# Hybrid trunk layer: another order of the query and key stage, part of its DMAs on POOL's queue, and the latents in eleven pieces

## Chip, core and metric

One core of a Trainium2 chip. The metric is the device time of one execution in microseconds, given as the median of three runs. TensorE is called PE, VectorE DVE, ScalarE ACT, GpSimd POOL and SyncE SP, as in the profile.

## What is computed

One layer with three branches (a Fourier mix, a gated delta rule scan, latent attention) that are merged by gates. The change touches the merge of the first two branches and the stage that makes queries, keys and values for the third. Cut to that:

```python
q = (rmsnorm(cq, q_norm) @ w_uq).reshape(B, L, 8, 64 + 32)      # cq: 1024 x 384
kv = (rmsnorm(ckv, kv_norm) @ w_ukv).reshape(B, L, 8, 64 + 64)  # ckv: (1024 + 256) x 256
q_nope, q_pe = q[..., :64], q[..., 64:]
k_nope, v = kv[..., :64], kv[..., 64:]
q_pe, kpe = apply_rope(q_pe, cos, sin), apply_rope(kpe, cos, sin)   # rope for the 1024, not the 256
# attention of 1024 queries over 1280 keys, 8 heads of 96
p = softmax(einsum('bqhd,bkhd->bhqk', q, k) * 96 ** -0.5)
merged = sigmoid(g_a) * (y_a @ w_branch[0]) + sigmoid(g_b) * (y_b @ w_branch[1]) + sigmoid(g_c) * (y_c @ w_branch[2])
```

All data is fp32. A product of two fp32 matrices is made of three matmuls on operands that are split into a high and a low part (high·high, high·low, low·high).

## The kernel before

**Order of work.** A planner orders the instructions of each engine from their dependencies and the program's order; it may let an instruction of a queue go ahead of one that stands earlier in the program. Where `self.fine` is true (the query and key stage and the attention), the matmuls keep the program's order, and so do the DVE instructions that are given to `pin`. Every engine and every DMA queue then works through its list in order: an instruction that waits holds up all behind it.

**Merge.** `merge_ab` runs m over eight tiles of the merged width. For each m it loads two weights (`wload`: SP loads, ACT makes the high part, POOL the low part), makes two products `pb` (b = 0 and 1, each 24 matmuls into one of two PSUM buffers), multiplies each by its gate on DVE (L1239; this frees the PSUM buffer), adds them on POOL (L1240) and stores the sum (L1241). At the end of m = 1 to 7 it takes one step of the generator `latents`, which prepares the third branch: `rows` (the norms' factors), the rope of the key's shared 32 dimensions (three pieces, stored in `kpd`), the normed key latents `ckh`/`ckl` and query latents `cqh`/`cql` (in `hilo`: DVE scales, ACT makes the high part, DVE the low part), and the values' weight. Each step issues its own loads into `cs` (three buffers) on SP's queue just ahead of the work on them.

**Query and key stage.** `qkv` makes tiles from the latents: `k_tile` (1280 columns in chunks of 512, 512 and 256; six matmuls a chunk), `qn_tile` (1024 columns in two chunks of nine matmuls), `qp_tile` (the rope part of the queries, four chunks of nine), `v_tile` (six matmuls). Each chunk of keys or queries goes through `put`: ACT copies the high part out of PSUM, DVE subtracts for the low part, and both are stored to DRAM, the high part from ACT's queue and the low part from SP's (L1366; four buffers `csh` and `csl`). From DRAM they come back in the layout of the attention: `k_pe` fills the shared 32 rows of the key tiles (one row of ones and eight DMAs, L1353 and L1357), `load_k` (L1424) and `load_q` (L1432, L1433) the others, all on SP's queue. `peak` makes one of the 20 pieces of the score maximum of the first query block: one matmul `s` into one of two PSUM buffers (two of half the width for the last four pieces), and one DVE maximum (L1448, L1454). `shift` joins them, and ACT writes the result into a row of the query tile (`Q<-sh`, L1466). The order before is: key tile 0, queries 0 (both parts), six value tiles, two maxima, key tile 1, three maxima, queries 1, four, key tile 2, three, queries 2, five, key tile 3, three, `shift`, queries' rope part 1, queries 3, four value tiles.

**Attention.** `attend` starts with the scores of the first block (`st<-Q,K`), and runs the maxima of the next block beside them; POOL adds up the weights.

Of the kernel before, what the change touches and what calls it, by code (L numbers as in the profile page):

```python
# [162 lines left out]
class K:  # L163
# [1023 lines left out]
    def merge_ab(self):  # L1187
        nc, tc, a = self.nc, self.tc, self.a
        with ExitStack() as es:
# [65 lines left out]
    def latents(self):  # L1255
# [3 lines left out]
        def cs(w):  # L1259
            return lp.tile([P, L], FP32, name="cs", bufs=3)[:, 0:w]  # L1260
# [15 lines left out]
        pieces = [(b, min(b + 512, LT)) for b in range(0, LT, 512)]  # L1276
        for b, e in pieces:
            w = e - b
            k = cs(2 * w)[0:32].rearrange("p (h c) -> p h c", h=2)
# [8 lines left out]
            hl = lp.tile([32, 2, 512], F32R, name="kphl", bufs=1)[:, :, 0:w]  # L1288
# [4 lines left out]
        self.ckh, self.ckl = (lp.tile([P, 2, LT], F32R, name=n) for n in ("ckh", "ckl"))  # L1293
        for b, w in ((0, L), (L, LC)):
            rb = cs(w)
            nc.sync.dma_start(out=rb, in_=rows[0][:, b:b + w].broadcast_to([P, w]))
            for k in range(2):
                st = cs(w)
                nc.sync.dma_start(out=st, in_=self.ckvd[k][:, b:b + w])
                self.hilo(st, self.kvn[:, k:k + 1], rb, self.ckh[:, k, b:b + w], self.ckl[:, k, b:b + w])  # L1300
            yield
        self.cqh, self.cql = (lp.tile([P, 3, L], F32R, name=n) for n in ("cqh", "cql"))
        rb = cs(L)
        nc.sync.dma_start(out=rb, in_=rows[1].broadcast_to([P, L]))
        for t in range(3):
            st = cs(L)
            nc.sync.dma_start(out=st, in_=self.cqd[t])
            self.hilo(st, self.qn_g[:, t:t + 1], rb, self.cqh[:, t, :], self.cql[:, t, :])
            if t == 0:
                yield  # L1310
        yield
        self.wvh, self.wvl = (lp.tile([P, 2, 512], F32R, name=n) for n in ("wvh", "wvl"))
        st = cs(L).rearrange("p (k c) -> p k c", k=2)
        nc.sync.dma_start(out=st, in_=self.a["wuv"])
        self.split(st, self.wvh, self.wvl)
        yield

    def qkv(self):
# [6 lines left out]
        with ExitStack() as es:  # L1325
# [3 lines left out]
            def cst(w):  # L1329
                return self.lp.tile([P, L], FP32, name="cs", bufs=3)[:, 0:w]  # L1330
# [56 lines left out]
            n = 0  # L1387

            def peaks(m):
                nonlocal n  # L1390
                for _ in range(m):
                    self.peak(0, n)
                    n += 1
# [23 lines left out]
            for t in range(VF, 10):  # L1417
                v_tile(t)
# [3 lines left out]
    def load_k(self, t):  # L1422
        for k, src in zip(self.Kt[t % 2], self.knd):
            self.nc.sync.dma_start(out=k[0:64].bitcast(FP32), in_=src[t].rearrange("(p d) l -> d p l", p=2))  # L1424

    def load_q(self, j):
# [4 lines left out]
        for q, n, p in zip(self.Qt[j], self.qnd, self.qpd):  # L1431
            nc.sync.dma_start(out=q[0:64].bitcast(FP32), in_=n[t].rearrange("(p d) l -> d p l", p=2)[:, :, bs])  # L1432
            nc.sync.dma_start(out=q[64:96].bitcast(FP32),  # L1433
# [35 lines left out]
    def attend(self):  # L1469
# [5 lines left out]
        with ExitStack() as es:  # L1475
# [58 lines left out]
            for j in range(NB):  # L1534
                more = j + 1 < NB
                n = 0
                if j % 2 == 0 and j + 2 < NB:
                    self.load_k(j // 2 + 1)
                if j + 2 < NB:
                    self.load_q(j + 2)  # L1540
# [131 lines left out]
```

## Time and profile before

| | us |
|---|---|
| median of three runs | 1612.68 (1611.36 to 1612.69) |
| profiled execution, its own time | 1606.86 |
| its span | 1605.1 |
| merge, first `pb` to last `pb` | 1014.6 to 1116.3 |
| query and key stage, to the first scores of the attention | 1116.7 to 1219.7 |
| PE busy over the span | 94% |
| mean granted clock of PE | 0.973 |

How to read it: PE is the engine with the most work, and the chain of work that ended last runs mostly over PE. A stage's time is PE's matmuls at the full clock, plus what PE waited, plus what the matmuls lost while the clock was granted at its lower level (half). The mean busy share hides this: a matmul at the lower level counts as busy all the same.

### The profile page before, as it was taken

To read this page: it belongs to the slowest core of one execution; us is meant where nothing else is said; L and a number is where in the kernel's file an instruction comes from. 1 tells how busy PE (TensorE), PEld (TensorE's weight loads), DVE (VectorE), ACT (ScalarE), POOL (GpSimd) and SP (SyncE) were. 2 spreads that over 40 slices of the span, in tenths; PEclk is the share of its full clock that TensorE was granted. 3 is DMA by queue.
4 is the path that set the end of the run, shared out by engine and by line. 5 is a ranking of instruction groups with operands and counts; after the bars stand their busy time and mean duration, and the time that the engine had idled before them with its cause. 6 is when DMAs were issued, how large, how long until landed. Compare 5 with 4: busy or idle time off the path is not lost.

```text
span 1605.1 us, 20192 instructions
## 1 busy us (share of the span) xinstructions
PE 1513.2 (94%) x7403; PEld 1185.2 (74%) x7403; DVE 794.1 (49%) x1489; ACT 545.1 (34%) x1158; POOL 564.4 (35%) x462
## 2 busy tenths in 40 slices
PE   6989999999899999999999999899679898999998
PEld 1676788888788878788788888777457565666886
DVE  2756665454343256345443123544245566756724
ACT  3455324322332433433432334122124343443311
POOL 0464242212235435443443221444005465653000
PEclk9899999999999999999999999999879999999999
DMA  8522222311332123224223226585862312103715
GB/s 322 164 59 74 83 69 88 121 47 67 118 96 92 56 73 118 77 74 144 57 86 108 77 79 209 165 282 183 217 203 86 76 30 60 27 14 125 230 37 180
DMA packets 93103, 179.35 MB, mean 112 GB/s; under 512 B 21510, under 2 KB 26568, under 8 KB 92748
## 3 DMA queue, kind: packets, MB, share of 16 engines
q1 hardware_dynamic: 81980, 158.82, 31.9%
q10 hardware_dynamic: 11024, 19.24, 3.3%
q8 instruction: 58, 0.95, 0.3%
q14 instruction: 41, 0.34, 0.1%
HBM read 125.60 MB, written 52.38 MB: 111 GB/s over the span
## 4 chain that ended last, share of the span: by engine, by line
PE 71%; DVE 6%; DMA 6%; issue 2%; ACT 2%; POOL 1%; SPq 1%; ACTq 0%; DVEq 0%; POOLq 0%
PE mm L175 31%; PE st L175 10%; PE pp L175 7%; PE pf L175 5%; PE g L175 5%; PE acc L175 4%; PE pb L175 3%; PE pm L175 2%; PE s L175 2%; DVE tmp L746 1%; DMA Q<-sh 1%; DMA ys<-in_wmod 1%; DMA Q<-qph 1%; PE g L182 1%; DVE N L748 1%
## 5 line engine op out<-in xcount | busy, mean ns | idle before, releaser
L197 POOL TENSOR_TENSOR wl<-wr,wh 128x512 fp32r<-128x512 f32 x142 | 195.8, 1380 | 544.6 <-ACT wh L196 527.7
L175 PE MATMUL mm<-hhi,wh 128*128 128x512 f32 x912 | 375.2, 411 | 1.4 <-ACT st L1075 1.0
L175 PE MATMUL mm<-hhi,wl 128*128 128x512 f32 x912 | 360.0, 395 | 0.0
L175 PE MATMUL mm<-hlo,wh 128*128 128x512 f32 x912 | 358.0, 393 | 0.0
L175 PEld LDWEIGHTS mm<-hhi,wl 128*128 128x128 f32 x912 | 172.1, 189 | 37.6
L175 PEld LDWEIGHTS mm<-hhi,wh 128*128 128x128 f32 x912 | 173.0, 190 | 32.7 <-ACT st L1075 1.4
L175 PEld LDWEIGHTS mm<-hlo,wh 128*128 128x128 f32 x912 | 173.2, 190 | 31.4 <-issue 0.8
L196 ACT CAST wh<-wr 128x512 fp32r<-128x512 f32 (+2 forms) x154 | 93.4, 608 | 202.4 <-PE mm L175 104.8
L175 PE MATMUL st<-Q,K 96*128 96x512 f32 (+1 forms) x480 | 139.6, 407 | 10.0 <-DMA Q<-sh 9.6
L1487 ACT ACTIVATE pf<-st 128x512 f32<-128x512 f32 x160 | 94.6, 597 | 130.1 <-PE st L175 127.6
L1448 DVE TENSOR_REDUCE mx<-s 128x1 f32<-128x512 f32 x128 | 86.6, 690 | 79.4 <-PE s L175 79.2
L175 PEld LDWEIGHTS st<-Q,K 96*128 96x128 f32 (+1 forms) x480 | 89.0, 193 | 45.3 <-DMA Q<-sh 12.4
L1496 POOL TENSOR_TENSOR sum<-sum,pf 128x512 f32<-128x512 f32 x94 | 117.8, 1284 | 3.2 <-ACT pf L1487 3.0
L175 PE MATMUL s<-K,Q 96*128 96x512 f32 (+1 forms) x192 | 63.5, 376 | 17.8 <-DMA Q<-qph 9.6
L175 PE MATMUL acc<-pf,V 128*64 128x512 f32 x320 | 72.2, 597 | 0.0
L175 PEld LDWEIGHTS s<-K,Q 96*128 96x128 f32 x192 | 36.7, 194 | 30.8 <-DVE mx L1448 11.1
L175 PE MATMUL pb<-yh,wh 128*128 128x512 f32 x128 | 51.8, 405 | 7.6 <-DVE t L1239 7.6
L878 POOL TENSOR_TENSOR Qm<-mk,Qf 128x128 f32<-128x128 f32 x64 | 31.9, 519 | 69.0 <-PE g L175 67.1
L175 PEld LDWEIGHTS acc<-pf,V 128*64 128x64 f32 x320 | 21.5, 136 | 42.1 <-issue 42.1
L869 DVE SCALAR_TENSOR_TENSOR S<-S,ex,g 128x128 f32<-128x128 f32 x48 | 15.2, 344 | 73.5 <-PE g L175 73.4
L175 PE MATMUL pb<-yh,wl 128*128 128x512 f32 x128 | 51.0, 398 | 0.0
L175 PE MATMUL pb<-yl,wh 128*128 128x512 f32 x128 | 51.0, 398 | 0.0
(392 smaller groups left out, 2725.9 us busy)
## 6 DMA issues: line engine op xcount, KB each, us to landing
wr<-in_win SPq DMA_DIRECT2D x118, 256.0 KB, 2.7
wm<-in_wmod SPq DMA_DIRECT2D x16, 512.0 KB, 7.0
tabd<-st ACTq DMA_DIRECT2D x24, 256.0 KB, 2.0
wr<-in_wbr SPq DMA_DIRECT2D x24, 256.0 KB, 4.4
t<-tabd SPq DMA_DIRECT2D x12, 512.0 KB, 3.9
xt<-in_xT SPq DMA_DIRECT2D x8, 640.0 KB, 10.9
wm<-in_win SPq DMA_DIRECT2D x8, 512.0 KB, 4.0
kqd<-lk SPq DMA_DIRECT2D x8, 512.0 KB
```

The costliest lines, as they stand in the source:

```text
L175: i = self.nc.tensor.matmul(out, lhsT, rhs, start=start, stop=stop)
L182: i = self.nc.tensor.transpose(out=out, in_=in_, identity=identity)
L196: nc.scalar.copy(out=hi, in_=raw)
L197: self.lo_eng.tensor_tensor(out=lo, in0=raw, in1=hi, op=ALU.subtract)
L746: nc.vector.tensor_tensor(out=tv, in0=XX[:, i:i + 1, i + 1:16].broadcast_to([P, m, m]), in1=N[:, i + 1:16, i + 1:16].rearrange("p k j -> p ...
L748: nc.vector.tensor_reduce(out=N[:, i, i + 1:16], in_=tv, axis=AX.X, op=ALU.add)
L869: nc.vector.scalar_tensor_tensor(out=Sn[:, dr], in0=S[:, dr], scalar=eL(dr), in1=sp[:, dr], op0=ALU.mult, op1=ALU.add)
L878: nc.gpsimd.tensor_tensor(out=Qm[:, dr], in0=self.mk[:, m_, :], in1=Qf[:, c[dr], :], op=ALU.mult)
L1448: self.pin(nc.vector.tensor_reduce(out=mx[:, i, c:c + 1], in_=ps, axis=AX.X, op=ALU.max))
L1487: nc.scalar.activation(out=pf, in_=ps, func=AF.Exp)
L1496: nc.gpsimd.tensor_tensor(out=out, in0=s[0], in1=pf, op=ALU.add)
```

## The change

- In the merge, a step of `latents` is taken at the end of every m and, from m = 1 on, another after the matmuls of b = 0, ahead of that product's gate on DVE. `latents` has eleven pieces of work in place of six, and each piece is followed by the issue of the next one's loads; `cs` has four buffers in place of three.
- In the query and key stage the order is: queries 0 (both parts), key tile 0, the shared key rows, the loads of key tile 0 and of query blocks 0 and 1, six value tiles; then for t = 1, 2, 3 key tile t, and for t = 1, 2 queries t, two value tiles and four maxima. `k_tile` and `qn_tile` make one maximum with each chunk, ahead of its `put`, while there are any. After `shift`: the queries' rope part 1, queries 3.
- The stores of the low parts, the eight DMAs and the row of `k_pe`, and these first loads of keys and queries are issued from POOL's queue in place of SP's. Later loads stay on SP's queue.

```diff
                     for c in range(2):
                         s = slice(c * 512, (c + 1) * 512)
                         self.mm3(ps[:, s], hi, lo, ...)
+                    if b == 0 and m:
+                        next(pieces, None)
                     nc.vector.scalar_tensor_tensor(out=g, in0=g, scalar=1.0, in1=ps, op0=ALU.add, op1=ALU.mult)
...
-                if m:
-                    next(pieces)
+                next(pieces, None)
...
+        def rope_load(b, e):
+            k = t["k", b] = cs(2 * (e - b))[0:32].rearrange("p (h c) -> p h c", h=2)
             if b < L:
                 nc.sync.dma_start(out=k, in_=self.kped.rearrange("(h p) l -> p h l", p=32)[:, :, b:e])
-                r = cs(2 * w)[0:32].rearrange("p (h c) -> p h c", h=2)
-                nc.sync.dma_start(out=r, in_=self.a["ropek"].rearrange("(h p) l -> p h l", p=32)[:, :, b:e])
-                nc.vector.tensor_tensor(out=k, in0=k, in1=r, op=ALU.mult)
-                nc.vector.tensor_tensor(out=k[:, 0], in0=k[:, 0], in1=k[:, 1], op=ALU.add)
+                t["r", b] = cs(2 * (e - b))[0:32].rearrange("p (h c) -> p h c", h=2)
+                nc.sync.dma_start(out=t["r", b], in_=self.a["ropek"].rearrange("(h p) l -> p h l", p=32)[:, :, b:e])
...
+        def row_load(i, b, w):
+            t["row"] = cs(w)
+            nc.sync.dma_start(out=t["row"], in_=rows[i][:, b:b + w].broadcast_to([P, w]))
+
+        def lat_load(src, key):
+            t[key] = cs(src.shape[-1])
+            nc.sync.dma_start(out=t[key], in_=src)
...
+        work = [(lambda b=b, e=e: rope_load(b, e), lambda b=b, e=e: rope_do(b, e)) for b, e in ((0, 512), (512, L), (L, LT))]
+        for b, w in ((0, L), (L, LC)):
+            for k in range(2):
+                load = lambda k=k, b=b, w=w: lat_load(self.ckvd[k][:, b:b + w], ("ck", k, b))
+                work.append((both(lambda b=b, w=w: row_load(0, b, w), load) if k == 0 else load,
+                             lambda k=k, b=b, w=w: ck_do(k, b, w)))
+        for k in range(3):
+            load = lambda k=k: lat_load(self.cqd[k], ("cq", k))
+            work.append((both(lambda: row_load(1, 0, L), load) if k == 0 else load, lambda k=k: cq_do(k)))
+        work.append((wv_load, lambda: self.split(t["wv"], self.wvh, self.wvl)))
+        work[0][0]()
         yield
...
+        for i, (_, do) in enumerate(work):
+            do()
+            if i + 1 < len(work):
+                work[i + 1][0]()
             yield
...
-                nc.sync.dma_start(out=self.Kt[1][0][KR:KR + 1].bitcast(FP32), in_=row)
+                nc.gpsimd.dma_start(out=self.Kt[1][0][KR:KR + 1].bitcast(FP32), in_=row)
...
-                            nc.sync.dma_start(out=self.Kt[b][i][64:KR, par].bitcast(FP32), in_=self.kpd[:, i])
+                            nc.gpsimd.dma_start(out=self.Kt[b][i][64:KR, par].bitcast(FP32), in_=self.kpd[:, i])
...
-                nc.sync.dma_start(out=dst[1][:, c:c + w], in_=lo.bitcast(FP32))
+                nc.gpsimd.dma_start(out=dst[1][:, c:c + w], in_=lo.bitcast(FP32))
 
             def k_tile(t):
                 for c, d, ps in up_tile(a["wuk"][t], 2, ckh, ckl, LT):
+                    peaks()
                     put(ps, [x[t] for x in self.knd], c)
 
             def qn_tile(t):
                 for c, d, ps in up_tile(a["wuq"][t], 3, cqh, cql, L):
+                    peaks()
                     put(ps, [x[t] for x in self.qnd], c)
...
-            k_tile(0)
             qn_tile(0)
             qp_tile(0)
+            k_tile(0)
             k_pe()
+            self.load_k(0, nc.gpsimd)
+            self.load_q(0, nc.gpsimd)
+            self.load_q(1, nc.gpsimd)
             for t in range(VF):
                 v_tile(t)
-                if t == 2:
-                    self.load_k(0)
-                    self.load_q(0)
-            peaks(2)
+            on = True
             for t in range(1, 4):
                 k_tile(t)
-                peaks(3)
-                if t == 1:
-                    self.load_q(1)
                 if t < 3:
                     qn_tile(t)
-                    peaks(4 if t == 1 else 5)
+                    for i in range(2):
+                        v_tile(VF + 2 * (t - 1) + i)
+                        peaks(2)
+            peaks(20)
             self.shift(0)
             qp_tile(1)
             qn_tile(3)
-            for t in range(VF, 10):
-                v_tile(t)
```

## Rows read from the trace of the kernel before

**Rows 1.** By stretch: us, busy us of PE, PEld, DVE, ACT, POOL, granted clock, DMA share, GB/s.
```profile
1014.60:1116.30 101.70, 94.12 (x391) 73.00 (x390) 49.11 (x50) 18.57 (x30) 42.76 (x24) 0.98 0.63 210
1116.30:1219.70 103.40, 80.28 (x302) 61.76 (x301) 42.44 (x66) 24.61 (x47) 8.71 (x5) 0.85 0.68 201
...
1140.99:1150.95 9.96, 0.33 (x2) 0.00 (x0) 0.00 (x0) 0.59 (x1) 0.00 (x0) 0.76 1.01 207
1150.95:1199.15 48.20, 35.04 (x116) 26.00 (x117) 24.09 (x41) 10.10 (x20) 0.00 (x0) 0.78 0.75 222
...
1219.70:1256.00 36.30, 36.30 (x160) 24.49 (x159) 22.46 (x34) 17.47 (x30) 22.27 (x18) 1.00 0.17 47
```
**Rows 2.** Waits in the merge, then in the stage: us, times, longest.
```profile
DVE cs L1251 <- DMA cs<-ckvd: 9.0, 2, 7.0
PE pb L175 <- DVE t L1239: 7.6, 4, 3.3
...
PE s L175 <- DMA Q<-qph: 9.6, 1, 9.6
PE s L175 <- DVE mx L1448: 6.5, 5, 1.7
PE st L175 <- ACT wh L196: 4.0, 1, 4.0
PE s L175 <- DVE mx L1454: 1.6, 1, 1.6
```
**Rows 3.** Chain of work in the stage: start us, us, what.
```profile
1116.67 16.04 PE st L175 x72
1132.70 1.40 PE acc L175 x6
...
1138.95 0.67 SPq L1424
...
1140.99 9.92 DMA Q<-qph
```
**Rows 4.** Timeline of PE: a chunk of 256 columns, and the transposition of `shift`.
```profile
1119.40 0.28 PE L175 MATMUL st<-ckl,wh 128*128 128x256 f32 x1
1119.52 0.28 PE L175 MATMUL st<-ckh,wl 128*128 128x256 f32 x1
...
1198.78 0.38 PE L182 MATMUL ms<-mk,m 128*8 128x128 f32 x1 [1.00 <-DVE m L1461]
```
**Rows 5.** Waits of SP's queue, 1014 us to 1222 us.
```profile
SPq L1366 <- DVE csl L1364: 37.3, 17, 6.0
```
**Rows 6.** Instructions of the low parts `csl`: time to landing.
```profile
DMA to landing us min/median/max: 2.0/3.6/4.3
```
**Rows 7.** DMA issues from 1116 us to 1160 us: sizes.
```profile
K<-knh SPq DMA_DIRECT2D x1, 640.0 KB
...
Q<-qnh SPq DMA_DIRECT2D x2, 256.0 KB
...
Q<-qph SPq DMA_DIRECT2D x2, 128.0 KB
```
**Rows 8.** Timeline of POOL, the stage's beginning: start us, us, what.
```profile
1120.71 2.23 POOL L1352 MEMSET K<- 1x2560 f32 x1
```
**Rows 9.** Instructions of the query tiles: time to landing.
```profile
DMA to landing us min/median/max: 3.9/5.8/9.7
```
**Rows 10.** By line in the stage: names, shapes xcount | busy us, mean ns | idle.
```profile
L1364 DVE TENSOR_TENSOR csl<-st,csh 128x512 fp32r<-128x512 f32 x16 | 11.0, 691 | 21.1 <-ACT csh L1363 19.5 <-DMA knl<-csl 1.5
L1448 DVE TENSOR_REDUCE mx<-s 128x1 f32<-128x512 f32 x16 | 10.4, 685 | 15.3 <-PE s L175 15.1
...
L197 POOL TENSOR_TENSOR wl<-wr,wh 128x512 fp32r<-128x512 f32 x3 | 3.9, 1293 | 92.6 <-ACT wh L196 92.6
```
**Rows 11.** Chain of work in the attention: a wait for the row that `shift` stores.
```profile
1273.02 8.22 DMA Q<-sh
```
**Rows 12.** Timeline of PE, merge: the first of its four waits.
```profile
1026.99 0.47 PE L175 MATMUL pb<-yh,wh 128*128 128x512 f32 x1 [1.00 <-DVE t L1239]
```

More of the change, by code (lines that the diff above doesn't have):

```diff
@@ L1259, in cs @@
         def cs(w):
-            return lp.tile([P, L], FP32, name="cs", bufs=3)[:, 0:w]
+            return lp.tile([P, L], FP32, name="cs", bufs=4)[:, 0:w]
         rows = []
@@ L1275, in latents, with rope_do @@
         yield
[L1276 to L1279, printed above, removed]
+        t = {}
+        def rope_load(b, e):
+            k = t["k", b] = cs(2 * (e - b))[0:32].rearrange("p (h c) -> p h c", h=2)
             if b < L:
                 nc.sync.dma_start(out=k, in_=self.kped.rearrange("(h p) l -> p h l", p=32)[:, :, b:e])
-                r = cs(2 * w)[0:32].rearrange("p (h c) -> p h c", h=2)
-                nc.sync.dma_start(out=r, in_=self.a["ropek"].rearrange("(h p) l -> p h l", p=32)[:, :, b:e])
-                nc.vector.tensor_tensor(out=k, in0=k, in1=r, op=ALU.mult)
-                nc.vector.tensor_tensor(out=k[:, 0], in0=k[:, 0], in1=k[:, 1], op=ALU.add)
+                t["r", b] = cs(2 * (e - b))[0:32].rearrange("p (h c) -> p h c", h=2)
+                nc.sync.dma_start(out=t["r", b], in_=self.a["ropek"].rearrange("(h p) l -> p h l", p=32)[:, :, b:e])
             else:
                 nc.sync.dma_start(out=k[:, 0], in_=self.kped[0:32, b:e])
-            hl = lp.tile([32, 2, 512], F32R, name="kphl", bufs=1)[:, :, 0:w]
+        def rope_do(b, e):
+            k = t["k", b]
+            if b < L:
+                nc.vector.tensor_tensor(out=k, in0=k, in1=t["r", b], op=ALU.mult)
+                nc.vector.tensor_tensor(out=k[:, 0], in0=k[:, 0], in1=k[:, 1], op=ALU.add)
+            hl = lp.tile([32, 2, 512], F32R, name="kphl", bufs=1)[:, :, 0:e - b]
             nc.scalar.copy(out=hl[:, 0], in_=k[:, 0])
@@ L1291, in latents @@
             nc.scalar.dma_start(out=self.kpd[:, :, b:e], in_=hl.bitcast(FP32))
-        yield
[L1293 to L1300, printed above, removed]
-            yield
@@ L1302, in latents @@
[L1302 to L1316, printed above, removed]
+        self.ckh, self.ckl = (lp.tile([P, 2, LT], F32R, name=n) for n in ("ckh", "ckl"))
+        self.cqh, self.cql = (lp.tile([P, 3, L], F32R, name=n) for n in ("cqh", "cql"))
+        self.wvh, self.wvl = (lp.tile([P, 2, 512], F32R, name=n) for n in ("wvh", "wvl"))
+        def row_load(i, b, w):
+            t["row"] = cs(w)
+            nc.sync.dma_start(out=t["row"], in_=rows[i][:, b:b + w].broadcast_to([P, w]))
@@ new lines, in lat_load, with ck_do, cq_do, wv_load @@
+        def lat_load(src, key):
+            t[key] = cs(src.shape[-1])
+            nc.sync.dma_start(out=t[key], in_=src)
+        def ck_do(k, b, w):
+            self.hilo(t["ck", k, b], self.kvn[:, k:k + 1], t["row"], self.ckh[:, k, b:b + w], self.ckl[:, k, b:b + w])
+        def cq_do(k):
+            self.hilo(t["cq", k], self.qn_g[:, k:k + 1], t["row"], self.cqh[:, k, :], self.cql[:, k, :])
+        def wv_load():
+            t["wv"] = cs(L).rearrange("p (k c) -> p k c", k=2)
+            nc.sync.dma_start(out=t["wv"], in_=self.a["wuv"])
@@ new lines, in both @@
+        def both(*fs):
+            return lambda: [f() for f in fs]
+        work = [(lambda b=b, e=e: rope_load(b, e), lambda b=b, e=e: rope_do(b, e)) for b, e in ((0, 512), (512, L), (L, LT))]
[4 more added lines that the diff above has]
+                             lambda k=k, b=b, w=w: ck_do(k, b, w)))
@@ L1329, in cst @@
             def cst(w):
-                return self.lp.tile([P, L], FP32, name="cs", bufs=3)[:, 0:w]
+                return self.lp.tile([P, L], FP32, name="cs", bufs=4)[:, 0:w]
             def v_tile(t):
@@ L1386, in qkv, with peaks @@
             self.Qt, self.mx = {}, {}
-            n = 0
-            def peaks(m):
+            n, on = 0, False
+            def peaks(m=1):
                 nonlocal n
                 for _ in range(m):
-                    self.peak(0, n)
-                    n += 1
+                    if on and n < 20:
+                        self.peak(0, n)
+                        n += 1
             self.fine = True
-            k_tile(0)
             qn_tile(0)
             qp_tile(0)
+            k_tile(0)
             k_pe()
+            self.load_k(0, nc.gpsimd)
+            self.load_q(0, nc.gpsimd)
+            self.load_q(1, nc.gpsimd)
             for t in range(VF):
                 v_tile(t)
-                if t == 2:
-                    self.load_k(0)
-                    self.load_q(0)
-            peaks(2)
+            on = True
             for t in range(1, 4):
                 k_tile(t)
-                peaks(3)
-                if t == 1:
-                    self.load_q(1)
                 if t < 3:
                     qn_tile(t)
-                    peaks(4 if t == 1 else 5)
+                    for i in range(2):
+                        v_tile(VF + 2 * (t - 1) + i)
+                        peaks(2)
+            peaks(20)
             self.shift(0)
@@ L1416, in qkv, with load_k, load_q @@
             qn_tile(3)
[L1417 to L1418 removed]
             self.fine = False
             self.lo_eng = nc.gpsimd
[L1422 removed]
+    def load_k(self, t, eng):
         for k, src in zip(self.Kt[t % 2], self.knd):
[L1424 to L1426 removed]
+            eng.dma_start(out=k[0:64].bitcast(FP32), in_=src[t].rearrange("(p d) l -> d p l", p=2))
+    def load_q(self, j, eng):
         nc, t, qb = self.nc, j // 2, j % 2
@@ L1537, in attend @@
                 if j % 2 == 0 and j + 2 < NB:
-                    self.load_k(j // 2 + 1)
+                    self.load_k(j // 2 + 1, nc.sync)
                 if j + 2 < NB:
-                    self.load_q(j + 2)
+                    self.load_q(j + 2, nc.sync)
                 for u in range(20):
```

4 lines of the change are left out of this document (2 added, 2 removed).

## Prediction

> **What bounds the kernel now.** I read the table of busy time by stretch first [rows 1]. In the merge PE is busy 94.1 of 101.7 us at a clock of 0.98. In the query and key stage it is busy 80.3 of 103.4 us at a mean clock of 0.85, while the attention's opening, 36.3 us, has PE busy throughout at 1.00. So the stage loses in two ways: PE waits, and then the clock is granted at the lower of its two levels. Next the table of waits [rows 2]: in the stage PE waits 9.6 us once for the query tile, 6.5 + 1.6 us for score maxima on DVE, and 4.0 us for a weight; in the merge 7.6 us, four times, for the gate on DVE (L1239). In the merge DVE in turn waits for loads (once 7.0 us for `ckvd`) with the gate queued behind.
>
> What PE has to do in the stage, at the full clock: the chain of waits shows its first 72 matmuls without a gap in 16.04 us, and a value tile of six in 1.40 us [rows 3]. A 512-column matmul is thus 0.233 us, and a 256-column one 0.12 us from start to start [rows 4]. A key tile (12 and 6) is 3.5 us, a `qn` tile (18) 4.2, a `qp` tile (36) 8.4, the maxima (16 and 8) 4.7. All of it: 4 x 3.5 + 4 x 4.2 + 2 x 8.4 + 10 x 1.4 + 4.7 = 66.3 us. From 1116.67 us to the first scores at 1219.7 us pass 103.0 us, so 36.7 are lost: 21.7 in the waits of rows 2, 1.0 in `shift` [rows 4], and some 14 to the clock, which is 0.6 us and more for each us waited.
>
> **The change part by part.** Count from the start of the stage.
>
> *Until the first maximum.* Queries 0 and key tile 0 are the same 72 matmuls, 16.0 us; six value tiles add 8.4, the first chunk of key tile 1 1.4: PE comes to the first maximum at 25.8 us. It needs key tile 0 and the high parts of query block 0, which pass through DRAM. Before, SP's queue stood 37.3 us in 17 waits for low parts [rows 5], and the load of the keys was issued only at 1138.95 us, 22.3 us into the stage, because the queries' rope part came last; its queries landed at 1150.9 us [rows 3]. Now the queries are through first and the keys' last chunk follows at 16.0 us. Its high and low part take ACT and DVE some 2 us (the rope sum stands ahead of them), the store lands 3.6 us later [rows 6], so the loads go at about 21.6 us. In the wait before, the DMA engines were full (share 1.01) and moved 207 GB/s, 2.06 MB in 9.96 us [rows 1]. Ahead of the last piece that counts go two times 640 KB of keys, 256 and 128 KB of queries [rows 7], 1.70 MB: 8.2 us. Ready at 29.8 us, a wait of 4.0; I take 4.5, since stores and weights of key tile 1 share the engines. Bounds: 0 (store landed in 2.0 us [rows 6], loads at a third more speed), and 7.8 (the 12.0 us that passed before from the keys' issue to the queries' landing [rows 3]). The clock lost with it, at 0.6 to 0.7 us for each us waited: 3.0.
>
> *POOL's queue.* Before the first maximum POOL issues seven stores of low parts, the row and eight shared-row DMAs, two key loads and two query loads: 20, of 43 in the stage. POOL's last work here is the memset of the row, 2.23 us from 1120.7 us [rows 8]; the planner can send the eight DMAs between the stores, as before. No DMA is issued from POOL in this trace. The nearest rows: SP's issue of such a load, 0.67 us [rows 3], and POOL's own work, 1.29 us for a subtraction [rows 10] and 2.23 us for the memset. POOL is free at 1122.9 us, 6.2 us in; 20 issues of price p and 5.8 us to landing [rows 9] give 12 + 20p us: 25 at 0.67, 37.8 at 1.29, 56.6 at 2.23. I take 0.9, as an issue does less than an elementwise pass: 30 us, no later than the 30.3 above, so no further term. The Trainium skill (DMA: Bandwidth & Descriptors, section SWDGE vs HWDGE vs iDMA, and its table of specifications) has software on POOL build the descriptors, with about 1 us to the first byte against 0.6 for SP and ACT; by 1 us, an estimate from that page, the first maximum is at 32 us and the total some 3 us later.
>
> *After it.* PE has 66.3 - 25.8 = 40.5 us left. A chunk with its maximum takes PE 1.40 + 0.23 = 1.63 us, and DVE a maximum of 0.69 and a low part of 0.69 [rows 10], 1.38 us: the maxima now hide behind chunks, where before they stood in runs of three to five against two PSUM buffers. The 6.5 + 1.6 us go. The weight's 4.0 us go too: its load was issued at SP behind low parts, which are no longer there. What can be late next: DVE waits for one of four `csl` buffers whose store lies behind POOL's loads, and the maximum behind it holds PE; a weight late on full DMA engines. I take 3.0 (0 to 8). `shift` keeps its 1.0.
>
> *At the end.* The four value tiles that ran between `shift` and the attention are gone from there; 54 matmuls, 12.6 us, now cover the row `Q<-sh`, which once in the attention took 8.2 us to land [rows 11], and the PSUM buffers of queries 3 wait for the rope sum and four low parts on DVE. I take 1.5 (0 to 6).
>
> The stage: 25.8 + 4.5 + 3.0 + 40.5 + 3.0 + 1.0 + 1.5 = 79.3 us against 103.0: **23.7 us gained**.
>
> *Merge.* To be had are the 7.6 us and, at 0.98 over 101.7 us, some 2 us of clock [rows 1, 2]. A step now comes every half of an m, 24 matmuls or 5.6 us, and its loads go one step ahead. The rope's loads fit; for `ckvd`, with a 7.0 us wait before, 5.6 us of lead and the slack of the second PSUM buffer, 5.6 less the gate's 1.2, suffice if SP's queue isn't held by the gates' loads. The first of the four waits, 1.0 us [rows 12], comes before DVE's first work on rope or latents and stays. I take **5.5 gained** (-3 to 9).
>
> Sum: 29.2. The profiled execution took 1606.86 us, span and 1.8 around it: 1577.7. The median lies 5.8 above it, so the forecast is 1612.7 - 29.2 = **1583 us**; its own range, with the terms at half of their bounds, 1574 to 1593.
>
> **The rivals.**
>
> *The DMA engines are the bound* (0.15). For: share 1.01 in the long wait, 0.68 of the whole stage, some 70 us of full transfer [rows 1], more than PE's 66. Against: 2 MB of it (keys 1, a later query block) may run into the attention, where the share is 0.17. Price: first maximum at 33.6 us, with some 24 of the 70 us of transfer done; the other 46 at a share of 0.82, between the 0.75 of the busier part and 1, take 56: 90 us, 13 gained, with 4 of the merge 1595 us. The Trainium skill (Trainium Kernel Development and Optimization, section Key Constraints) puts it as a rule: queues of several engines share the same 16 DMA engines, so another queue saves only issue time. By that rule alone moving the loads to POOL gains nothing in the full stretch; the waits of SP's queue [rows 5] speak for some gain outside it.
>
> *POOL's issue is dear but below break-even* (0.11). At 1.29 us the first maximum comes at 37.8 us, 12 us waited and 8 lost to the clock: 37.8 + 8 + 40.5 + 5.5 = 92 us, 11 + 5.5 gained: 1596 us. At 2 us, 1610.
>
> *POOL's issue is the bound: slower* (0.10). Everything behind the first maximum waits for POOL. The stage is 12 + 20p + 54 us; with the merge's 5.5 it is even at 108.5, p = 2.1 us. For: the memset's 2.23 us lies beyond that. Against: 1.29 us for a whole subtraction. At 2.5 us: 116 us, 13 lost less 5.5: 1620 us.
>
> *The pieces hold up the merge* (0.05). A piece now stands ahead of the gate of b = 0. Five of them waiting 2 us beyond the slack cost 10 in place of 5.5 gained: 1599 us.
>
> *The order isn't what the program says* (0.04). Only matmuls and maxima keep it; if the planner lets loads wait behind later stores on POOL, the first wait is as before and only the other waits go: within 0.2%, 1610 us.
>
> **How the numbers follow.** Forecast 0.55. The range takes in the DMA bound, a POOL price to 1.8 us and the favourable ends: 1571 to 1606. A measurement tells 0.2%, some 3.2 us. Faster: 0.55 + 0.15 + 0.09 of the dear issue + 0.05 = 0.84; same 0.06; slower 0.10.
>
> **What would show it.** In the profile after: the first `s` waits 3 to 8 us for a query or key load, some 30 us into the stage; no wait of PE for `mx` over 1 us; none for `wh`; clock above 0.92 in the stage; the stage some 79 us; POOL issues of about 0.9 us, 43 of them; in the merge one wait for the gate of about 1 us and no load waited for by DVE over 2 us. Wrong it is if POOL's issues are over 1.5 us, if the DMA share is near 1 throughout the stage with PE waiting for weights or `csl`, or if `Q<-sh` holds the attention's first scores.

## The result and the profile after

The changed kernel takes **1594.52 us** (median of four runs, 1592.14 to 1596.81) against 1612.02 us (1609.12 to 1612.69) for the kernel before in the same session: 0.9892 times, with a 95% interval of 0.9862 to 0.9921. It is faster by 1.1%, inside the range of 1571 to 1606 us, and 11.5 us slower than the forecast of 1583: of 29.2 us that were to be gained, 17.5 came.

Where the profiled executions differ (spans 1605.1 and 1590.4 us; "first maximum" is the first matmul `s`, the last column the attention and all behind it):

| us | ahead of the merge | merge | stage to the first maximum | from there to the first scores | rest |
|---|---|---|---|---|---|
| before | 1014.6 | 101.9 | 34.5 | 68.7 | 385.4 |
| after | 1022.5 | 98.1 | 42.5 | 43.4 | 383.9 |
| forecast | 1014.6 | 96.4 | 30.3 | 49.0 | 385.4 |

The gain behind the first maximum is larger than forecast, the merge's (3.8 us, forecast 5.5) is somewhat smaller, and the time to the first maximum, which was to fall by 4.2 us, rose by 8.0. The busy time by stretch of the kernel after answers to [rows 1]: us, busy us of PE, PEld, DVE, ACT and POOL, granted clock, DMA share, GB/s.

```profile
1022.50:1120.60 98.10, 94.31 (x392) 73.28 (x391) 50.01 (x48) 18.81 (x31) 45.16 (x24) 0.98 0.64 213
1120.60:1206.50 85.90, 70.16 (x301) 56.47 (x300) 38.97 (x63) 22.72 (x45) 28.57 (x43) 0.90 0.78 230
1120.60:1151.00 30.40, 27.91 (x115) 21.84 (x113) 11.34 (x18) 9.40 (x19) 14.06 (x20) 0.94 0.74 229
1151.00:1163.10 12.10, 0.00 (x0) 0.00 (x0) 0.69 (x1) 0.26 (x1) 5.04 (x10) 0.61 1.04 231
1163.10:1206.50 43.40, 42.25 (x186) 34.63 (x187) 26.94 (x44) 13.07 (x26) 9.46 (x15) 0.95 0.74 231
```

Line three is PE's work up to the first maximum, line four the wait for it, line five all that follows, in which PE is busy for 42.25 of 43.40 us. The waits of PE in the stage, and two of POOL's, answer to [rows 2] (us, times, longest):

```profile
PE s L175 <- DMA Q<-qph: 12.5, 1, 12.5
PE st L175 <- DVE cs L1405: 1.9, 1, 1.9
PE ms L182 <- DVE m L1485: 1.1, 1, 1.1
...
POOL knl L1389 <- DVE csl L1387: 18.2, 9, 5.0
POOL qpl L1389 <- DVE csl L1387: 10.8, 1, 10.8
```

The waits for maxima (6.5 and 1.6 us) and for the weight (4.0 us) are gone. The one wait that was expected, for the first loads, is 12.5 us in place of 4.5, and a new one stands ahead of it: 1.9 us for `cs`, the product of the queries with the rope table. The chain of work tells what both rest on (start us, us, what):

```profile
1124.73 0.33 SPq L1243
1125.10 7.25 DMA rope<-in_rope
1132.38 0.70 DVE cs L1405
1133.12 3.90 PE st L175 x9
...
1144.81 5.42 DMA knl<-csl
1150.27 0.48 issue
1150.77 0.58 POOL K L1448
1151.35 0.39 POOL Q L1456
1151.93 11.07 DMA Q<-qph
1163.13 0.77 PE s L175
```

The load of the rope table stands on the chain: it was issued 4.5 us into the stage, where before it was issued at 974.1 us, long ahead. And POOL's queue, in order of time (start us, us, line, what, [idle before]):

```profile
1126.94 1.30 POOL L1389 DMA_DIRECT2D qnl<-csl  x2
1128.23 0.51 POOL L1376 DMA_DIRECT2D K<-K  x1
1128.73 1.46 POOL L1380 DMA_DIRECT2D K<-kpd  x3
1141.02 1.16 POOL L1389 DMA_DIRECT2D qpl<-csl  x2 [10.82 <-DVE csl L1387]
1142.58 1.14 POOL L1389 DMA_DIRECT2D knl<-csl  x2 [0.40 <-DVE csl L1387]
1143.70 0.51 POOL L1380 DMA_DIRECT2D K<-kpd  x1
1144.81 0.56 POOL L1389 DMA_DIRECT2D knl<-csl  x1 [0.59 <-DVE csl L1387]
1145.37 1.96 POOL L1380 DMA_DIRECT2D K<-kpd  x4
1147.89 0.59 POOL L1448 DMA_DIRECT2D K<-knh  x1 [0.56 <-DMA knh<-csh]
1150.77 0.59 POOL L1448 DMA_DIRECT2D K<-knl  x1 [2.29 <-DMA knl<-csl]
1151.34 0.59 POOL L1456 DMA_DIRECT2D Q<-qnh  x1
1151.93 0.54 POOL L1457 DMA_DIRECT2D Q<-qph  x1
```

An issue takes some 0.5 to 0.6 us (1.96 us are four; the longest of the stage, a first store, 0.75), so POOL is not short of time: it waits. For 10.8 us it stood at the low part of the queries' rope half, with five of the eight shared-row DMAs behind; those then went out right ahead of the keys. The first keys were issued 27.3 us into the stage (1147.89 - 1120.6), forecast 21.6. The queries stood on the same queue behind the low part of the keys, for whose store POOL waited another 2.29 us, and then took 11.07 us to land. From the keys' issue to the queries' landing (1163.0) passed 15.1 us.

### The profile page after: what moved, and what is told of

Read it like the earlier page. It is cut to its first block, busy times and chain, and to the rows that moved or that the text cites. A ratio compares the mean times of both kernels' runs of the same rounds, so it can differ in the third digit from the quotient of the medians.

```text
span 1590.4 us, 20204 instructions
## 1 busy us (share of the span) xinstructions
PE 1509.4 (95%) x7403; PEld 1185.1 (75%) x7403; DVE 795.4 (50%) x1489; ACT 544.7 (34%) x1158; POOL 588.8 (37%) x505
## 4 chain that ended last, share of the span: by engine, by line
PE 70%; DMA 8%; DVE 6%; issue 2%; POOL 2%; ACT 2%; SPq 1%; DVEq 0%; POOLq 0%; ACTq 0%
PE mm L175 31%; PE st L175 9%; PE pp L175 7%; PE pf L175 5%; PE g L175 5%; PE pb L175 4%; PE acc L175 3%; PE s L175 2%; PE pm L175 2%; DMA Q<-sh 2%; DVE tmp L746 1%; DMA ys<-in_wmod 1%; DMA Q<-qph 1%; DVE N L748 1%; PE g L182 1%
## 5 line engine op out<-in xcount | busy, mean ns | idle before, releaser
L175 PEld LDWEIGHTS st<-Q,K 96*128 96x128 f32 (+1 forms) x480 | 88.6, 193 | 44.6 <-DMA Q<-sh 12.6
L175 PE MATMUL s<-K,Q 96*128 96x512 f32 (+1 forms) x192 | 62.3, 367 | 12.7 <-DMA Q<-qph 12.5
L175 PEld LDWEIGHTS acc<-pf,V 128*64 128x64 f32 x320 | 21.6, 136 | 42.1 <-issue 42.1
L175 PE MATMUL pb<-yh,wh 128*128 128x512 f32 x128 | 51.5, 402 | 1.5 <-DVE t L1241 1.5
L782 POOL TENSOR_TENSOR Ym<-Y,mk 128x512 f32<-128x512 f32 x30 | 38.7, 1291 | 35.1 <-PE pp L175 30.3
```

What stands on the lines that cost most here:

```text
L175: i = self.nc.tensor.matmul(out, lhsT, rhs, start=start, stop=stop)
L782: nc.gpsimd.tensor_tensor(out=Ym, in0=Y, in1=off.broadcast_to(sh), op=ALU.mult)
```

## The experiments

Ratios are to the kernel before in the same session: its median was 1612.86 us for the first four experiments, 1605.84 us for the next four and 1607.91 us for the last four. The columns are those of the table above; all are profiles of one execution.

| | us | ratio, 95% | ahead | merge | to first maximum | on to scores | stage |
|---|---|---|---|---|---|---|---|
| e1 rope table early | 1592.09 | 0.9864 [0.9831, 0.9896] | 1021.9 | 98.5 | 38.8 | 43.7 | 82.5 |
| e2 shared rows on SP | 1590.79 | 0.9854 [0.9823, 0.9885] | 1022.6 | 97.7 | 38.5 | 43.8 | 82.3 |
| e3 all on SP | 1602.51 | 0.9927 [0.9900, 0.9954] | 1027.9 | 96.7 | 41.4 | 51.5 | 92.9 |
| e4 merge as before | 1597.07 | 0.9901 [0.9870, 0.9932] | 1025.5 | 104.0 | 38.8 | 43.8 | 82.6 |
| e5 = e1 + e2 | 1578.56 | 0.9832 [0.9805, 0.9858] | 1017.4 | 97.7 | 33.1 | 42.6 | 75.7 |
| e6 merge alone | 1605.42 | 1.0005 [0.9981, 1.0029] | 1025.3 | 97.1 | 39.3 | 63.9 | 103.2 |
| e7 more cover | 1584.92 | 0.9867 [0.9837, 0.9898] | 1023.4 | 96.5 | 43.7 | 40.7 | 84.4 |
| e8, e10, e11 before again | | | 1018.0, 1016.9, 1014.7 | 100.9, 104.1, 103.5 | 34.5, 34.3, 35.1 | 69.3, 66.3, 63.5 | 103.8, 100.6, 98.6 |
| e9 = e5 + e7 | 1578.31 | 0.9811 [0.9776, 0.9846] | 1020.1 | 100.0 | 33.2 | 38.6 | 71.8 |
| e12 after again | | | 1019.4 | 97.3 | 43.5 | 43.5 | 87.0 |

**The rope table (e1).** Its tile is taken from the latents' pool, so that its place is free early; nothing else is edited.

```diff
-            rope = up.tile([P, 2, L], FP32, name="rope")
+            rope = self.lp.tile([P, 2, L], FP32, name="rope")
```

> The changed kernel with the rope table in the pool of the latents, so that its load is issued in the merge and not at the stage's beginning (1125.1 us in the profile after, landed 1132.4 us). Theory 1 (a chain of waits: rope table late, queries' rope part late, keys' low parts late, first loads late): PE's 1.9 us wait for the rope product goes, the keys are asked for some 2 us earlier in the stage, the first maximum waits 10 to 11 us in place of 12.5, stage 82 to 84 us in place of 86, median 2 to 4 us below the changed kernel. Theory 2 (the DMA engines are full and only the bytes count): 1 MB less in the stage at 231 GB/s is 4.5 us, the first maximum waits some 8 us, median 6 to 8 us below.

PE now comes to the first maximum after 26.2 us (38.8 less a wait of 12.6); the forecast had 25.8. So the late table is what PE's arrival lacked, and it moved the whole of the loads with it: the wait keeps its size, 12.6 us, where the first theory had 10 to 11. That the table was late through the merge's half of the change is seen in two other runs: with the old stage and the new merge (e6) it was issued at 1126.9 us, with the new stage and the old merge (e4) at 985.0 us. That it is the fourth `cs` buffer in that half, and not the eleven pieces, is argued and not shown: no run moves the buffer alone.

**The shared rows (e2).** The row of ones and the eight DMAs of `k_pe` go back to SP's queue.

```diff
-                nc.gpsimd.dma_start(out=self.Kt[1][0][KR:KR + 1].bitcast(FP32), in_=row)
+                nc.sync.dma_start(out=self.Kt[1][0][KR:KR + 1].bitcast(FP32), in_=row)
...
-                            nc.gpsimd.dma_start(out=self.Kt[b][i][64:KR, par].bitcast(FP32), in_=self.kpd[:, i])
+                            nc.sync.dma_start(out=self.Kt[b][i][64:KR, par].bitcast(FP32), in_=self.kpd[:, i])
```

> The changed kernel with the row and the eight DMAs of the shared key rows on SP's queue in place of POOL's. In the profile after five of these eight stood behind two low parts for which POOL's queue waited 10.8 us, and were issued at 1143.7 to 1147.3 us, just ahead of the first key load. Theory 1 (the wait at the head of POOL's queue held them back, and they then ran beside the first loads): all eight are issued by 1135 us, in a stretch in which the DMA engines have room; 0.8 MB less runs beside the first loads and the key load goes 2 us earlier; the first maximum waits 6 to 8 us in place of 12.5, median 6 to 9 us below the changed kernel. Theory 2 (the sum of bytes sets the first maximum): the same bytes have to pass, first wait 11.5 to 13.5 us, median within 2 us of the changed kernel.

The wait falls to 6.6 us and is now for the keys:

```profile
PE s L175 <- DMA K<-knh: 6.6, 1, 6.6
PE st L175 <- DVE cs L1405: 3.2, 1, 3.2
```

The median, 1590.79 us, was not the 6 to 9 us below the changed kernel's that were expected, and the eight DMAs were issued from 1127.4 to 1145.1 us, not by 1135. The run also moves more than its diff says. With the rows gone from POOL's queue, the planner put the queries' loads between the low parts' stores, ahead of the keys (`Q<-qnh` from 1134.96 us, in the changed kernel from 1151.34). Which of the two, the 1280 KB of rows (eight times 160 KB) out of the way or the queries' early start, brings how much, it can't say.

**All of it on SP (e3).** Every DMA that the change moved to POOL is issued from SP again; the new order stays.

```diff
-                nc.gpsimd.dma_start(out=dst[1][:, c:c + w], in_=lo.bitcast(FP32))
+                nc.sync.dma_start(out=dst[1][:, c:c + w], in_=lo.bitcast(FP32))
...
-            self.load_k(0, nc.gpsimd)
-            self.load_q(0, nc.gpsimd)
-            self.load_q(1, nc.gpsimd)
+            self.load_k(0, nc.sync)
+            self.load_q(0, nc.sync)
+            self.load_q(1, nc.sync)
```

The row and the eight DMAs of `k_pe` go to SP as in e2.

> The changed kernel with every DMA that it moved to POOL's queue back on SP's: order, maxima and merge stay changed. If the queue matters (SP's queue again waits for low parts with weights' loads behind them): PE waits for weights 4 us or more, stage 4 to 8 us longer than the changed kernel's 86, median 4 to 8 us above it. If all queues share the same DMA engines and another queue saves issue time alone: stage within 1.5 us of 86, median within 2 us.

```profile
PE s L175 <- DMA Q<-qph: 10.8, 1, 10.8
PE st L175 <- ACT wh L196: 4.5, 1, 4.5
PE st L175 <- DVE cs L1405: 2.7, 1, 2.7
...
SPq L1389 <- DVE csl L1387: 28.3, 16, 6.4
```

To the first maximum POOL's queue brings nothing (41.4 against 42.5 us); behind it it brings 8 us. The weight's wait is back, 4.5 us, with SP's queue at a stand for low parts, as in [rows 2, 5]; the rest of the 8 us is the clock, 0.88 behind the first maximum in place of 0.95. This is read from one profile of e3, of its longest execution; the ratios of e3 and of the changed kernel overlap. So in the stage the move pays by what no longer queues behind a waiting store, not by time of issue. The rule of the Trainium skill that the prediction weighed (Trainium Kernel Development and Optimization, section Key Constraints: another engine's queue saves only issue time) does not hold for these 8 us.

**The merge as before (e4), and alone (e6).** The one keeps the new stage with the old `merge_ab`, `latents` and three buffers, the other the new merge with the old stage.

```diff
-                    if b == 0 and m:
-                        next(pieces, None)
...
-                next(pieces, None)
+                if m:
+                    next(pieces)
...
-            return lp.tile([P, L], FP32, name="cs", bufs=4)[:, 0:w]
+            return lp.tile([P, L], FP32, name="cs", bufs=3)[:, 0:w]
```

> The changed kernel with the merge and its latents as before the change (seven steps, each with its own loads, three buffers); the query and key stage stays changed. Two effects: the merge from its first to its last product goes from 97.9 us back to about 101.8, and with three buffers the rope table's load is early again, as before the change, which by theory 1 gives the stage 2 to 4 us back and by theory 2 six or more. So median within 2 us of the changed kernel by theory 1, 2 to 4 us below it by theory 2.

For e6 the other half of the change's diff is taken back:

```diff
-            qn_tile(0)
-            qp_tile(0)
             k_tile(0)
+            qn_tile(0)
+            qp_tile(0)
...
-            self.load_k(0, nc.gpsimd)
-            self.load_q(0, nc.gpsimd)
-            self.load_q(1, nc.gpsimd)
...
-                nc.gpsimd.dma_start(out=dst[1][:, c:c + w], in_=lo.bitcast(FP32))
+                nc.sync.dma_start(out=dst[1][:, c:c + w], in_=lo.bitcast(FP32))
```

> The kernel before with the changed merge and latents alone (eleven pieces, four buffers); the query and key stage as before. If the merge's gain is its own, it goes from the 101.9 us of the profile before (104.0 in the run with the old merge) to 97.5 to 98.5 us. The rope table's load is late here too (four buffers), but the first rope product comes 3.5 us later than in the changed order, so it costs the stage 0 to 2 us against its 103.2. Median 2 to 6 us below the kernel before.

PE's waits for the gate are 7.0 us with the old merge and 2.2 us with the new one, and the merge is 104.0 and 97.1 us long. Yet e6 as a whole gains nothing that can be measured. Its profile has the merge's 4.8 us, an unchanged stage of 103.2 us, and 1025.3 us ahead of the merge in place of 1014.6. In the same way e4 is 2.5 us slower than the changed kernel's first figure, across sessions, which decides nothing. The nearest pair is e1 and e4, of one session: their stages are alike (82.5 and 82.6 us), their merges 98.5 and 104.0 us long, and their medians lie 5.0 us apart, but the intervals of their ratios overlap. The merge's gain is shown in its stretch, and not in the time.

**Both repairs (e5).**

> Both edits that shortened the stage singly, together: the rope table loaded in the merge, and the shared key rows on SP's queue. Singly they brought the first maximum from 42.5 us after the stage's beginning to 38.8 and 38.5 us. If they are two separate links of one chain (theory 1) the gains add: first maximum at 34 to 36 us, PE there at 26, a wait of 8 to 10 us, stage 78 to 80 us. If both gave no more than room on the DMA engines (theory 2), the second adds little, as the engines then are no longer full: first maximum at 37 to 38.5 us, stage 81 to 82.5 us.

The first maximum comes at 33.1 us after a wait of 3.2 us for the first keys: 9.4 us sooner than in the changed kernel, more than the 3.7 and 4.0 us of e1 and e2 added. Why more than the sum is not shown; as in e2, the planner sent the queries' loads ahead of the keys here (`Q<-qnh` from 1124.15 us). The time is 0.9832 times that of before, better than the change as it is (0.9892, in another session; the two intervals just miss each other). By stretch (up to the first maximum, and on to the scores), and what ACT and DVE waited for ahead of the keys' last chunk:

```profile
1115.10:1148.20 33.10, 27.71 (x116) 21.99 (x114) 12.32 (x19) 9.52 (x19) 15.15 (x20) 0.95 0.87 258
1148.20:1190.80 42.60, 40.99 (x187) 33.18 (x188) 27.22 (x44) 13.29 (x26) 9.06 (x14) 1.00 0.77 240
```
```profile
1135.28 0.37 ACT L1386 CAST csh<-st 128x256 fp32r<-128x256 f32 x1 [2.78 <-DMA qph<-csh]
...
1136.74 0.42 DVE L1387 TENSOR_TENSOR csl<-st,csh 128x256 fp32r<-128x256 f32 x1 [3.41 <-DMA qpl<-csl]
```

PE was through with that chunk at 1131.15 us, 16.0 us into the stage. Its high part was made by 1135.65 and its low part by 1137.16 us, 4.5 and 6.0 us later, since each had to wait for one of its four buffers to be stored. The prediction had some 2 us here. ACT's stand also held up the copy of a value tile, for which PE waited 2.1 us; PE came to the first maximum after 29.9 us, expected at 26.

**More cover (e7, e9).** All ten value tiles stand ahead of the first maximum, and the maxima follow two by two behind chunks and tiles of queries; e7 does this to the changed kernel, e9 to e5.

```diff
-                    peaks()
+                    peaks(2)
                     put(ps, [x[t] for x in self.qnd], c)
...
-            for t in range(VF):
+            for t in range(10):
...
-                    for i in range(2):
-                        v_tile(VF + 2 * (t - 1) + i)
-                        peaks(2)
+                    peaks(2)
```

> The changed kernel with all ten value tiles ahead of the first maximum in place of six; the eight maxima that stood behind value tiles stand two to a chunk of queries and two after each query tile. Four value tiles are 5.6 us of matmuls. If the first maximum is set by when the first loads land (theories 1 and 2), it stays at 42 to 43 us and its wait falls from 12.5 to some 7 us; what follows it is 5.6 us shorter: stage 79.5 to 81.5 us. If PE itself sets it (the wait moves along), it comes at 48 us and the stage stays at 86 us. The maxima, closer together, may add 0 to 2 us of waits for DVE.

> The changed kernel with the rope table taken from the latents' pool (its load early), the keys' shared rows on SP's queue, and with more of PE's work ahead of the first maximum (ten value tiles there, then two maxima behind each key tile). Without the cover, these two moves gave a first maximum 33.1 us into the stage, of which 3.2 us were a wait for the first keys, and a stage of 75.7 us. Theory (what is left of the wait is a transfer that has its own time, so PE's work put into it comes for nothing): the first maximum begins 33 to 35 us into the stage, waits under 1 us, first maximum to first attention score falls from 42.6 to 39.5 to 40.5 us, the stage takes 73 to 75 us, 1575 to 1578 us in all. Rival (the loads start from what PE has already done, in the order in which it is written, so work put ahead of them delays them by as much): the wait stays near 3 us, the first maximum begins 35 to 37 us into the stage, the stage stays at 75 to 77 us and the time at 1577 to 1581 us.

In e7 the wait falls from 12.5 to 7.1 us, and the first maximum stays near where it was (43.7 against 42.5 and 43.5 us): the loads don't follow PE. But the stage, 84.4 us, misses the 79.5 to 81.5 that were expected. From there to the scores only 2.7 us came off in place of 5.6: PE's matmuls there fell from 42.25 to 37.95 us of busy time, and its waits grew. The ratios of e7 and of the changed kernel overlap. In e9 the wait for loads is gone, and the stage, of 71.8 us (expected 73 to 75), is PE's work and little else; by stretch, up to the first maximum and on to the scores, and then all waits of PE in it:

```profile
1120.10:1153.30 33.20, 31.36 (x139) 25.43 (x138) 11.62 (x18) 11.28 (x22) 14.59 (x19) 1.00 0.88 260
1153.30:1191.90 38.60, 35.90 (x163) 28.46 (x162) 27.30 (x45) 11.34 (x23) 9.69 (x15) 1.00 0.83 262
```
```profile
PE acc L175 <- ACT V L1360: 1.8, 1, 1.8
PE s L175 <- DVE mx L1470: 1.4, 2, 0.8
PE ms L182 <- DVE m L1483: 1.1, 1, 1.1
```

At the full clock all through, 71.8 us stand against the 66.3 us of matmuls that the prediction worked out. Its median is that of e5, however (1578.31 and 1578.56 us in different sessions, ratios whose intervals overlap): the 3.9 us of stage between them are not shown in the time.

**What stands ahead of the merge (e8, e10 to e12).** Kernel before and kernel after again, unchanged, for the start of the merge.

> The kernel before once more, for a second profile. In its first profile the merge began at 1014.6 us; in the profiles of the changed kernel and of its four variants it began at 1021.9 to 1027.9 us, though the instructions ahead of it are the same. If that is how single executions differ, it begins at 1014 to 1028 us here too, with a stage of 102 to 104 us; if the changed kernel slows what stands ahead of the merge, it is 1014 to 1016 us again.

> The kernel before, for its profile: does the time that its merge's first product begins at vary by itself? It was 1014.6 and 1018.0 us in two profiles of it and 1017.4 to 1027.9 us in eight profiles of changed kernels, whose instructions ahead of there are the same in kind and order. Theory (it varies by itself, with the short stretches at the lower granted clock near 221 and 583 us that come and go): 1015 to 1025 us here, with a stretch below 1.00 at 220 to 235 us in at least one of the two profiles of this call. Rival (something in the change makes it later, by the memory's layout): 1014 to 1019 us in both, and a granted clock of 1.00 at 220 to 235 us in both.

> The kernel before, for its profile, as the run before this one. Theory (varies by itself): merge's first product between 1015 and 1025 us, and the two profiles apart by some us. Rival (the change's memory layout makes it later): 1014 to 1019 us and no stretch below 1.00 at 220 to 235 us.

> The changed kernel, for its profile. Theory (the part ahead of the merge varies by itself): merge's first product between 1015 and 1025 us. Rival (the change makes it later): 1020 to 1028 us again, and the granted clock falls again at 220 to 235 us. Either way the stage is expected as in its first profile: first maximum 40 to 44 us into it, with a wait of 10 to 14 us for the first queries or keys, and a stage of 83 to 88 us.

Four profiles of before reach the merge at 1014.6 to 1018.0 us, ten of the other kernels at 1017.4 to 1027.9; only one of the ten (e5) lies among those of before. The program there is the same, and the traces hold 5129 or 5130 matmuls in all of them. What differs most is short stretches at a lower mean clock; PE's waits there add up to some 42 to 44 us in the profiles of before and 43 to 45 in the others. Here are 220 to 235 us, in the kernel before, after, and after again, and behind them 110 to 125 us of before and of e8, one kernel in two executions:

```profile
220.00:235.00 15.00, 14.07 (x95) 12.35 (x94) 9.62 (x17) 3.77 (x9) 7.35 (x5) 1.00 0.14 46
```
```profile
220.00:235.00 15.00, 14.75 (x79) 13.14 (x80) 6.62 (x14) 4.10 (x9) 4.05 (x3) 0.77 0.15 54
```
```profile
220.00:235.00 15.00, 13.73 (x88) 11.95 (x88) 9.71 (x17) 5.14 (x10) 6.15 (x5) 1.00 0.15 54
```
```profile
110.00:125.00 15.00, 13.43 (x78) 11.62 (x79) 9.21 (x22) 11.24 (x26) 4.06 (x4) 1.00 0.31 88
```
```profile
110.00:125.00 15.00, 13.46 (x61) 11.27 (x61) 8.65 (x21) 11.08 (x25) 3.28 (x3) 0.77 0.26 78
```

They come and go in one and the same kernel, so they vary by themselves. But at 220 to 235 us all four profiles of before stand at 1.00 and nine of the ten others at 0.77, e4 and e6 with half of the change each among them; the tenth is the changed kernel again (e12), at 1.00. So this stretch goes with the changed programs, though not in every execution; what they share that brings it is open. Of the expectations, the theory that the start varies by itself held in e8 (1018.0 us) and e12 (1019.4); in e10 and e11 (1016.9 and 1014.7 us, both at 1.00 there) the rival held, that the change makes it later, and the stretch below 1.00 that the theory wanted was missing. The profiles of before lie 4.9 us lower than the two of after (means of 1016.1 and 1021.0 us).

## Why the prediction was right or wrong

The direction was right, the size was 0.6 of what was forecast. By the prediction's own steps:

**Until the first maximum: wrong, 30.3 us forecast, 42.5 measured, outside the wait's bounds of 0 to 7.8 us.** Three things failed in it.
- *PE arrives at 25.8 us.* It arrived at 30.0. The merge's half of the change was read as a matter of the merge alone; with it the rope table was loaded late (by the argument above, since a fourth `cs` buffer decides when the table's place comes free). PE waited 1.9 us for `cs`, with the clock's loss behind it. With the table early it is 26.2 us (e1).
- *The loads go at 21.6 us, with 1.70 MB ahead.* They went at 27.3 us. The late table is 3.7 us of that (e1). The shared rows were taken to run between the stores "as before"; but five of the eight waited behind POOL's 10.8 us stand and then went out ahead of the keys, 0.8 MB that the sum did not have. With both repaired the first keys are issued at 25.9 us and the first maximum comes at 33.1 us, 2.8 us from the forecast (e5). These last 2.8 us lie on the way of the keys' high part: it is made 4.5 us after PE in place of 2 (the buffers of `put`), its store lands 5.3 us later in place of 3.6, and its load takes 7.2 us in place of 8.2 and the 0.5 added.
- *8.2 us for the transfer.* It took 15.1 us from the first keys' issue to the queries' landing, 2.3 of them POOL's wait for the low part's store with the queries behind it. The rate, 237 GB/s at a share of 1.04, is above the 207 of [rows 1]. What the sum lacked was bytes in the way: 3.6 MB moved in these 15.1 us, where it had 1.70:

```profile
1147.89:1163.00 15.11, 2.75 (x12) 1.89 (x11) 0.69 (x1) 1.76 (x3) 5.77 (x11) 0.69 1.04 237
```

**The clock, 3.0 us for 4.5 us waited: wrong in kind.** By that price 12.5 us of waiting would have cost 8; behind it PE ran 43.4 us at 0.95, some 2 us lost. In the kernel before 48.2 us behind a wait of 9.6 us ran at 0.78 [rows 1], and there the waits for maxima and the weight came one behind the other. Nor do the waits alone set the loss: the four profiles of before have the same waits in the stage, within 0.7 us each, and from the first maximum on the clock was 0.81, 0.81, 0.82 and 0.89 (below, the first and the last of the four). So a price per us waited does not carry over from one order to another; why the clock stayed low behind the short waits is not shown. The stage's clock, 0.90, falls below the 0.92 that was named because of the wait itself (0.61 in it).

```profile
1151.00:1219.70 68.70, 55.31 (x192) 41.93 (x193) 31.56 (x50) 16.01 (x31) 3.88 (x3) 0.81 0.63 193
1153.30:1216.80 63.50, 49.79 (x192) 37.86 (x193) 31.52 (x50) 15.95 (x31) 3.89 (x3) 0.89 0.67 208
```

**After the first maximum: right, and better than forecast.** 43.4 us against 49.0 (3.0 of clock, 40.5, 3.0, 1.0 and 1.5). No wait for a weight, 0.2 us for a maximum. The 3.0 us for `csl` or weights and the 1.5 us at the end were not needed; `shift` cost 1.1. POOL's queue is 8.1 of the 25.3 us gained here, by the one profile of e3 (51.5 us without it); the rest came with the order.

**POOL's price: too high, without harm.** 0.54 us for an issue (median of the low parts' stores) where 0.9 was taken and 0.67 was the lowest row. The other term of that sum was read too low: the 5.8 us to landing of [rows 9] are taken over the whole execution, while the load on the chain took 9.92 us before [rows 3] and 11.07 after; with 9.92, 0.9 us an issue would have given 34 us in place of 30. The two errors pull in opposite ways. Both rivals of a dear POOL fall with it; the 1 us worked out beside it from the Trainium skill (DMA: Bandwidth & Descriptors) is no closer, though it names the first byte and not the issue. The rival that the planner's order differs (0.04) did not come true as it was priced: the first loads went out ahead of the later stores.

**The merge: right.** 98.1 and 97.3 us against a mean of 102.6 over four profiles of before: 4.9 us, forecast 5.5. One or two waits for the gate, 1.5 and 2.1 us in all (the changed kernel and again). DVE does wait for loads for over 2 us (once 3.7 for `cqd`), against what was named, but PE doesn't see it.

**The rival of the DMA engines as the bound gave 1595 us, and 1594.5 was measured; it is not what happened.** It had the first maximum at 33.6 us and then 56 us of transfers at a share of 0.82. The engines were full in the wait for the first maximum (1.04), and the 43.4 us behind it ran at a mean share of 0.74 with PE busy nearly throughout. In e9 the same transfers, but for the rope table's 1 MB, run beside PE's work at a share of 0.85 over 71.8 us, and PE waits for none of them directly: what was lacking was their order. The number agrees by chance.

**Not in the prediction at all:** the part ahead of the merge, 4.9 us longer by the means, with the stretch at 220 us in it. With it, the stage's 15.1 us (a mean of 101.6 over four profiles of before against 86.5 over two), the merge's 4.9 and -0.7 in the rest, the profiles gain 14.4 us and the medians 17.5.

## What to carry to other kernels

Before a queue takes over several kinds of DMA, write its list down in order and look for the first entry that waits for a late producer: whatever stands behind it, however early its own data, goes out in a burst ahead of the load that matters. A change to one stage can make a load of the next one late, as the new merge did with the rope table, so look up for each load of the next stage what frees its place. And where a load's time is fixed by what was issued before it, put independent matmuls into the wait: in e7 that took 5.4 us from the wait and moved its end by 1.2 us at most, though only 2.7 us came off behind it, and in e9, with the loads in order, 4.0 us against e5.

## What the runs showed of the hardware that was not expected

- The same DMA cost as much to issue from POOL's queue as from SP's, or more (medians, SP in the kernel before): loads of keys 0.59 against 0.58 us, shared rows 0.50 against 0.42, stores of the keys' low parts 0.54 against 0.34. What the move to POOL gained was not the price of an issue.
- A load's time to landing changed with what ran beside it: 9.92 us for the query load on the chain before, in a stretch with a share of 1.01; 6.3, 11.1 and 11.7 us (least, median, most) for the query loads issued from 1145 to 1162 us after, mostly at a share of 1.04; 4.4, 5.3 and 8.4 us for those of e9, issued from 1129 to 1149 us in a stretch of 33.2 us with a share of 0.88.
- One long wait of PE, 12.5 us, cost less of the granted clock behind it (0.95 over 43.4 us) than a wait of 9.6 us with several short ones behind it did before (0.78 over 48.2 us); without a wait for loads (e9) the stage ran at 1.00.
- Stretches at a lower mean clock in a part of the program that the edit doesn't touch came and went between executions of one kernel (110 to 125 us: 1.00, 0.77, 0.89 and 1.00 in the four profiles of before); the start of the merge differed by up to 3.4 us between these four, and by 3.1 us between the two of the changed kernel.
